# Four products in one PSUM bank without side sums, the second norm between the early products, the residual by another queue

## The chip, the cores and the metric

The kernel runs on one core of one Trainium2 chip. Its time is the device time of one launch in microseconds (us). TensorE (PE) multiplies, VectorE (DVE) and ScalarE (ACT) work on tiles and empty PSUM, GpSimd (POOL) does little, and SyncE (SP) issues the DMAs.

## The reference

Two layers over 1024 latent tokens of width 1024 (and 256 context tokens that layer 0 reads). Each layer is a mixer and then a channel MLP of hidden width 4096, both on a modulated norm and added to the stream with a gate:

```
x = x + g1 * mixer(modulate(rms_norm(x, n1), sh1, sc1))
x = x + g2 * sq_relu_mlp(modulate(rms_norm(x, n2), sh2, sc2), w1, w2)

def sq_relu_mlp(h, w1, w2):
    return jnp.square(jax.nn.relu(h @ w1)) @ w2
```

The mixer of layer 0 is retention beside softmax attention with shared keys and values; that of layer 1 is a gated MLP (`z = gelu(h @ w_in)`, `u, v = z`, `v` normed and mixed within chunks of 128 positions by a 128x128 matrix per group, then `(u * sv) @ w_out`). All is float32.

## The kernel before, in words

**Numbers.** Each float32 operand is split into a high part that PE takes and the rest (`split`: ACT casts the high part, DVE subtracts for the low part), and each product of two 128-wide tiles is three matmuls (`mm3`, lines 68 to 70): high by high, high by low, low by high. Tokens stand in the free dimension in two halves of 512 (`hf` 0 and 1).

**The channel MLP** (`layer_mlp`, line 903) replaces eight block products of a 2 by 2 blocked matrix product by seven. Activations come in seven forms (B11, T2, B21, T3, T1, T4, B22: halves of the tokens, and sums and differences of them), weights in seven (A11, S2, A12, S3, S1, A22, S4), which `w_forms` makes on DVE and ACT from two raw loads. A product (`block`) of four 128-wide tiles is 12 matmuls into one PSUM bank of 512 columns. There are eight banks in use as a ring.

`norm_forms` makes the normed activations: for half 0 the forms B11 and B21, for half 1 the other five, in four steps of the tile pairs t. It is a generator: `later` queues it, each `tick()` runs one step, `drain()` the rest. Half 0's steps run between the output projection's tiles of half 1. `up_first` then makes two products, A11 B11 and A12 B21, for the first eight of the 16 hidden blocks p (banks `uf`; results `ef`, `sf` go to DRAM by tiles of the ring `t`, four buffers that the norm uses too), and `drain()` after it runs half 1's norm. `mlp_up` makes the remaining products of each p in banks `ua`, `ub`, `ue`; seven forms of the result go to DRAM (`s_d`), and `mlp_down` loads them again and makes jobs (q, p0 to p1): q is one of four output block rows, a job takes one to four p. It accumulates into the residual tiles `xd` (the stream before the MLP, loaded from DRAM) by `scalar_tensor_tensor` on DVE; A11 B11, which three outputs share, is summed apart in a tile `acc` and added to three outputs in the last job of each q. The last three jobs, of p 13, 14 and 15, have three, two and one p. `done` then squares and sums the finished rows for the next norm, or writes the output.

**Queues and order.** All DMAs are issued on SP. Raw weights pass through three staging tiles of 512 KB, forms through a ring of 11 tiles `wr`. When the program is built, a scheduler sets each engine's order, which so differs from the code's in places; on the chip each engine runs its own in order and waits by semaphores.

Of the kernel before, what the change touches and what calls it, by code (L numbers as in the profile page):

```python
# [16 lines left out]
P = 128  # L17
D = 1024
KT = D // P
T = 1024  # L20
# [7 lines left out]
NW = 11  # L28
# [4 lines left out]
def hybrid_retention_gqa_chunkmlp_kernel(tc, I, out):  # L33
# [9 lines left out]
    stage, close_stage = open_pool("stage", bufs=3)  # L43
# [17 lines left out]

    def w_tile():

        wnext[0] += 1
        return wring[wnext[0] % NW]

# [9 lines left out]
    def load_w(src, name, eng=nc.vector):  # L76
        st = stage.tile([P, WCOL], F32, tag="st", name=f"st_{name}")
# [45 lines left out]
    def mod_steps(todo):  # L123
        for l, part in todo:
            acc = mpool[0].tile([P, D], F32, tag="macc", bufs=1, name=f"macc{l}{part}")
            for k in range(KT):
                st = stage.tile([P, WCOL], F32, tag="st", name=f"mw{l}{part}{k}")
# [432 lines left out]
    nt, close_nt = open_pool("nt")  # L560
    yf_pool, close_yf = open_pool("yf")
# [7 lines left out]
    def att_load(G, hh):  # L569
        if hh == 0:  # L570
# [4 lines left out]
            for dst, src in ((akc, ak_d[G, :, 0:TC]), (av[:, :, 0:1024], avd[:, 0:1024]), (av[:, :, 1024:], avd[:, 1024:])):  # L575
                st = stage.tile([P, WCOL], F32, tag="st", name=f"ast{G}")[:, :src.shape[-1]]
# [100 lines left out]
    def w_form(src, name, eng=nc.vector):  # L677
        w = src.shape[-1]
        t = w_tile().rearrange("p (a b) -> p a b", a=2)
        split(src, t[:, 0, :w], t[:, 1, :w], eng)  # L680
        return t

    def w_raw(src, name):
        n = src.shape[-2]
        r = stage.tile([P, WCOL], F32, tag="st", name=name)[:, :2 * n * P]
# [4 lines left out]
    def w_forms(src, name, skip=False, eng=nc.vector):  # L690
# [5 lines left out]
        if not skip:  # L696
            f["A11"] = w_form(R1[:, 0], f"w0_{name}")
        s1 = tmp(f"s1_{name}")[:, :w]
        eng.tensor_tensor(s1, R2[:, 0], R2[:, 1], ALU.add)
        s2 = tmp(f"s2_{name}")[:, :w]  # L700
        eng.tensor_tensor(s2, s1, R1[:, 0], ALU.subtract)
        f["S2"] = w_form(s2, f"w1_{name}")
        if not skip:
            f["A12"] = w_form(R1[:, 1], f"w2_{name}")
        eng.tensor_tensor(R2[:, 0], R1[:, 0], R2[:, 0], ALU.subtract)
        f["S3"] = w_form(R2[:, 0], f"w3_{name}")
        f["S1"] = w_form(s1, f"w4_{name}")
        f["A22"] = w_form(R2[:, 1], f"w5_{name}")
        eng.tensor_tensor(R1[:, 1], R1[:, 1], s2, ALU.subtract)
        f["S4"] = w_form(R1[:, 1], f"w6_{name}")  # L710
# [60 lines left out]
    def mlp_up(l, F, s_d, utemp, pro):  # L771
# [3 lines left out]
        for p in range(16):  # L775
# [9 lines left out]

            e1, s11 = utemp(f"e1_{l}_{p}"), utemp(f"s11_{l}_{p}")
            if p in pro:
# [8 lines left out]
            if p not in pro:  # L796
                block(a, f["A12"], F["B21"], False)
                nc.scalar.activation(s11, a, AF.Relu)
                nc.scalar.activation(s11, s11, AF.Square)
                put("B11", s11)  # L800
            block(b, f["S3"], F["T3"], False)
            u3 = utemp(f"u3_{l}_{p}")
            nc.vector.tensor_tensor(u3, b, e1, ALU.add)
            block(e, f["S1"], F["T1"], True)
            nc.vector.tensor_tensor(u3, e, u3, ALU.add)
            act(u3)
            put("B22", u3)
            block(b, f["A22"], F["T4"], False)
            nc.vector.tensor_tensor(e1, b, e1, ALU.add)
            act(e1)  # L810
# [9 lines left out]
            put("T3", u2)  # L820
            t4 = utemp(f"q4_{l}_{p}")
            nc.vector.tensor_tensor(t4, e1, t2, ALU.subtract)
            put("B21", e1)
            put("T4", t4)

    def up_first(l, F, s_d, e_d):

        for p0 in range(0, NPRO, 2):
# [17 lines left out]
    def mlp_down(l, xt, acc, s_d, done):  # L846
        S = {}
        sums = set()
# [10 lines left out]
        def job(q, p0, p1):  # L859
# [5 lines left out]
            f = w_forms(lambda i: I["w2"][l, q, i, :, :, p0:p1], name)  # L865
# [16 lines left out]
            block(a, f["A12"], F["B21"], False)  # L882
            stt(x11, a, g1)
            block(b, f["S3"], F["T3"], False)
            stt(x22, b, g2)
            block(e, f["S1"], F["T1"], True)
            stt(x22, e, g2)
            block(b, f["A22"], F["T4"], False)
            stt(x21, b, g2)
            block(e, f["S4"], F["B22"], False)  # L890
            stt(x12, e, g1)
# [7 lines left out]
        job(3, 0, 3)  # L899
        for i in range(16):  # L900
            job(i % 4, i, min(i + 4, 16))

    def layer_mlp(l, F, close_xt, s_d, e_d, x1_d, done):
# [9 lines left out]
        xt = [xd.tile([P, T], F32, name=f"xd{l}_{m}") for m in range(KT)]  # L913
        for m in range(KT):
            nc.sync.dma_start(xt[m], x1_d[m])
        acc = xd.tile([P, 4, H], F32, name=f"acc{l}")
        mlp_down(l, xt, acc, s_d, lambda q: done(q, xt))
        return close_xd, xt
# [20 lines left out]
    def done0(q, xt):  # L939
        if not ss1:  # L940
            ss1.extend(norm_tmp(0, 1))
        for m in (q, q + 4):
            for hf in range(2):
                norm_acc(nt, ss1[hf], xt[m][:, hf * H:(hf + 1) * H], m == 0, nc.vector)
            nc.sync.dma_start(xp_d[m], xt[m])

    close_xd, xt = layer_mlp(0, F, close_xa, s_d, e_d, x1_d, done0)
    hm = [[None] * KT for _ in range(2)]
    for hf in range(2):
        rs = norm_rstd(nt, ss1[hf], H)  # L950
# [20 lines left out]
    for cg in range(2):  # L971
        W = [load_w(I["wv"][cg, 2 * j:2 * j + 2].rearrange("k p n -> p k n"), f"wv{cg}_{j}") for j in range(4)]
        for tt in range(NTT):
            hf, o = tt // 4, (tt % 4) * P
            ps = mm_tile([P, 4, P], f"pv{cg}_{tt}")
            for k in range(KT):
                wc = slice((k % 2) * H, (k % 2) * H + H)
                mm3(ps.rearrange("p a b -> p (a b)"), hm[hf][k][:, 0, o:o + P], hm[hf][k][:, 1, o:o + P],
                    W[k // 2][0][:, wc], W[k // 2][1][:, wc], k == 0, k == KT - 1)
            for j in range(4):  # L980
                nc.scalar.activation(zg[cg * 4 + j][:, tt, :], ps[:, j, :], AF.Gelu_apprx_tanh)
# [12 lines left out]
    yg = [[None] * 8 for _ in range(2)]  # L994
    for g in range(8):
        W = load_w(I["wu"][g].rearrange("p k j -> p (k j)"), f"wu{g}")
        nc.vector.tensor_tensor(zg[g], zg[g], vr.unsqueeze(2).broadcast_to([P, NTT, P]), ALU.mult)
        for hf in range(2):
# [4 lines left out]
            pv = aux_tile([P, 4, P], f"psv{g}_{hf}")  # L1003
            for j in range(4):
                nc.tensor.matmul(pv[:, j, :], lhsT=zg[g][:, hf * 4 + j, :], rhs=wsT[:, g, :], start=True, stop=True)
            sv = tmp("sv").rearrange("p (a b) -> p a b", b=P)
            nc.vector.scalar_tensor_tensor(sv, pv, gains[:, 4, g:g + 1],
# [102 lines left out]
```

## Time and profile before

| | us |
|---|---|
| median of three runs (lowest, highest) | 2441.57 (2439.18, 2442.20) |
| the profiled execution | 2442.82 |
| its span, first to last instruction | 2440.5 |
| PE busy | 2248.6 (92%) |
| DVE busy | 1681.8 (69%) |
| ACT busy | 1021.3 (42%) |
| POOL busy | 123.8 (5%) |

Mean granted TensorE clock: 0.966 of full speed. Busy times are sums over the whole span, and the stages differ: in the up and down stages PE works nearly without a pause, and between stages it waits. A wait's releaser is the instruction whose end released the waiting one.

### The profile page before, as it was taken

How to read it: one execution, taken by the hardware profiler on the slowest of the kernel's cores; microseconds unless marked ns; L12 is line 12 of the kernel's file. 1: busy time of each engine (PE TensorE's matmuls, PEld its weight loads, DVE VectorE, ACT ScalarE, POOL GpSimd, SP SyncE). 2: the span in 40 equal slices, each digit the busy share in tenths (PEclk: the TensorE clock that was granted, in tenths of full speed). 3: DMA queues.
4: the chain of work that ended last, by engine and by line, in shares of the span. 5: the costliest groups of instructions: out<-in, count | busy, mean ns of one | idle time of the engine just before them, and what ended most of it. 6: DMA issues, size and time to landing. Idle time of an engine off the chain costs nothing. (4 is left out here: it accounts for less than half of the span.)

```text
span 2440.5 us, 28880 instructions
## 1 busy us (share of the span) xinstructions
PE 2248.6 (92%) x10412; PEld 1805.8 (74%) x10412; DVE 1681.8 (69%) x2798; ACT 1021.3 (42%) x1813; POOL 123.8 (5%) x101
## 2 busy tenths in 40 slices
PE   6998999799998699998999959999949999899998
PEld 1887787588886578876777838788837788677786
DVE  4657668689762977668878672444558766798886
ACT  3511122288644544554444233322445454544441
POOL 2223231000000000000000000000000000000000
PEclk9999999899999899999999969999979999999999
DMA  8245556410353464456444231115516544745442
GB/s 286 75 138 161 171 156 198 145 64 27 109 169 128 152 206 160 151 199 211 151 148 149 77 123 53 52 35 183 158 69 217 187 154 135 278 148 153 150 138 85
DMA packets 157407, 350.70 MB, mean 144 GB/s; under 512 B 16336, under 2 KB 30160, under 8 KB 157264
## 3 DMA queue, kind: packets, MB, share of 16 engines
q1 hardware_dynamic: 157264, 348.86, 44.3%
q8 instruction: 81, 1.33, 0.2%
q14 instruction: 62, 0.51, 0.1%
HBM read 262.29 MB, written 86.51 MB: 143 GB/s over the span
## 5 line engine op out<-in xcount | busy, mean ns | idle before, releaser
L68 PE MATMUL ub<-T,wr 128*128 128x512 f32 x384 | 153.8, 402 | 61.2 <-ACT wr L73 58.7
L68 PE MATMUL dbd<-sT,wr 128*128 128x512 f32 x384 | 155.9, 406 | 29.2 <-DVE xd L872 17.6
L68 PE MATMUL pl<-wr,h 128*128 128x512 f32 x384 | 154.1, 401 | 0.2 <-ACT zrl L477 0.2
L70 PE MATMUL dbd<-sT,wr 128*128 128x512 f32 x384 | 154.1, 401 | 0.0
L69 PE MATMUL dbd<-sT,wr 128*128 128x512 f32 x384 | 153.8, 400 | 0.0
L70 PE MATMUL ub<-T,wr 128*128 128x512 f32 x384 | 153.3, 399 | 0.0
L69 PE MATMUL ub<-T,wr 128*128 128x512 f32 x384 | 153.1, 399 | 0.0
L70 PE MATMUL pl<-wr,h 128*128 128x512 f32 x384 | 152.3, 397 | 0.0
L69 PE MATMUL pl<-wr,h 128*128 128x512 f32 x384 | 151.7, 395 | 0.0
L68 PEld LDWEIGHTS ub<-T,wr 128*128 128x128 f32 x384 | 73.1, 190 | 83.1 <-ACT wr L73 60.6
L73 ACT CAST wr<-ra_d 128x512 fp32r<-128x512 f32 (+3 forms) x114 | 62.4, 553 | 124.7 <-PE dbd L69 59.0
L68 PEld LDWEIGHTS dbd<-sT,wr 128*128 128x128 f32 x384 | 73.3, 191 | 53.9 <-DVE xd L872 20.0
L872 DVE SCALAR_TENSOR_TENSOR xd<-dbd,mcol,xd 128x512 f32<-128x512 f32 x114 | 85.2, 748 | 37.7 <-PE dbd L70 25.1
L132 DVE SCALAR_TENSOR_TENSOR macc<-mw,scc,macc 128x1024 f32<-128x1024 f32 x70 | 91.7, 1310 | 23.2 <-DMA mw<-in_mod_w 22.6
L68 PE MATMUL dad<-sB,wr 128*128 128x512 f32 x256 | 102.8, 402 | 5.2 <-ACT acc L878 3.4
L70 PE MATMUL dad<-sB,wr 128*128 128x512 f32 x256 | 101.6, 397 | 0.3 <-DVE wr L74 0.2
L69 PE MATMUL dad<-sB,wr 128*128 128x512 f32 x256 | 101.7, 397 | 0.0
L74 DVE TENSOR_TENSOR sT<-sT 128x512 fp32r<-128x512 f32 x128 | 87.4, 687 | 19.7 <-ACT sT L73 19.3
L73 ACT CAST sT<-sT 128x512 fp32r<-128x512 f32 x128 | 78.7, 619 | 48.5 <-DMA sT<-s_d 46.2
L70 PEld LDWEIGHTS dbd<-sT,wr 128*128 128x128 f32 x384 | 73.4, 191 | 18.9 <-DVE wr L74 1.1
L70 PEld LDWEIGHTS ub<-T,wr 128*128 128x128 f32 x384 | 72.9, 190 | 18.8 <-DVE wr L74 1.3
L69 PEld LDWEIGHTS dbd<-sT,wr 128*128 128x128 f32 x384 | 73.5, 192 | 16.5
(354 smaller groups left out, 6224.8 us busy)
## 6 DMA issues: line engine op xcount, KB each, us to landing
s_d<-ur SPq DMA_DIRECT2D x208, 256.0 KB, 2.2
mw<-in_mod_w SPq DMA_DIRECT2D x96, 512.0 KB, 4.5
sT<-s_d SPq DMA_DIRECT2D x128, 256.0 KB, 3.6
sB<-s_d SPq DMA_DIRECT2D x96, 256.0 KB, 2.7
st_wo<-in_wo SPq DMA_DIRECT2D x32, 512.0 KB, 3.9
ra_u<-in_w SPq DMA_DIRECT2D x32, 512.0 KB, 4.2
rb_u<-in_w SPq DMA_DIRECT2D x32, 512.0 KB, 3.8
ra_d<-in_w SPq DMA_DIRECT2D x26, 512.0 KB, 5.2
```

Of the source, the lines that this page charges most:

```text
L68: nc.tensor.matmul(ps, lhsT=a_hi, rhs=b_hi, start=first, stop=False, skip_group_check=more)
L69: nc.tensor.matmul(ps, lhsT=a_hi, rhs=b_lo, start=False, stop=False, skip_group_check=more)
L70: nc.tensor.matmul(ps, lhsT=a_lo, rhs=b_hi, start=False, stop=last, skip_group_check=more)
L73: nc.scalar.copy(hi, src)
L74: eng.tensor_tensor(lo, src, hi.bitcast(F32), ALU.subtract)
L132: nc.vector.scalar_tensor_tensor(acc, st, scc[:, k, 0:1], acc, ALU.mult, ALU.add)
L872: nc.vector.scalar_tensor_tensor(o, ps_, g, o, ALU.mult, ALU.add)
```

## The change

- The ring of weight forms has 12 tiles. Staging tiles are taken from a ring written out by hand, three, and a fourth from the attention on. The tile `acc` is gone.
- `up_first` calls `tick()` after each early product, so half 1's norm steps stand between the early products.
- `mlp_up`: for the eight p without early products, A11 B11, S2, S3 and A22 go into one bank (`ub`) in a chain, and the partial sums are copied out by ACT between them. The order of the forms is A11, A12, S2, S1, S3, S4, A22.
- `mlp_down`: the same chain; each partial sum is added to one output on its way, so no sum is kept apart. Half 0 of a row is finished (`done(q, 0)`) before half 1. For p 13 to 15 the S1 and S4 products are returned (`left`) and run later: in layer 0 between the two halves' norms, in layer 1 at the end.
- The residual is loaded on POOL's queue, and the residual for layer 1's mixer is written there in halves; the output is written in halves by SP.
- Layer 1's mixer: the first four tiles of `v` are summed with the input block outside, and the gate of `u` runs one product late.

```diff
@@ up_first
             for d in range(2):
                 block(ps[d], W[d][0], F["B11"], True)
+                tick()
                 e1 = tmp(f"ef{l}_{p0 + d}")
                 nc.scalar.copy(e1, ps[d])
                 nc.sync.dma_start(e_d[p0 + d], e1)
             for d in range(2):
                 block(ps[d], W[d][1], F["B21"], False)
+                tick()
@@ mlp_up
-                block(a, f["A11"], F["B11"], True)
-                nc.scalar.copy(e1, a)
-            block(b, f["S2"], F["T2"], True)
+                block(b, f["A11"], F["B11"], True)
+                nc.scalar.copy(e1, b)
+                block(a, f["A12"], F["B21"], True)
+                nc.vector.tensor_tensor(s11, a, e1, ALU.add)
+                act(s11)
+                put("B11", s11)
+            block(b, f["S2"], F["T2"], early)
             u2 = utemp(f"u2_{l}_{p}")
-            nc.vector.tensor_tensor(u2, b, e1, ALU.add)
...
+            if early:
+                nc.vector.tensor_tensor(u2, b, e1, ALU.add)
+            else:
+                nc.scalar.copy(u2, b)
+            block(e, f["S1"], F["T1"], True)
...
@@ mlp_down, job
-            block(a, f["A11"], F["B11"], True)
-            if q in sums:
-                nc.vector.tensor_tensor(acc[:, q, :], a, acc[:, q, :], ALU.add)
-            else:
-                nc.scalar.copy(acc[:, q, :], a)
-                sums.add(q)
-            block(b, f["S2"], F["T2"], True)
+            def p5():
+                block(e, f["S1"], F["T1"], True)
+                stt(x22, e, g2)
+
+            def p3():
+                block(e, f["S4"], F["B22"], False)
+                stt(x12, e, g1)
+                if p1 == 16:
+                    done(q, 1)
+
+            block(b, f["A11"], F["B11"], True)
+            stt(x11, b, g1)
+            block(a, f["A12"], F["B21"], True)
+            stt(x11, a, g1)
+            block(b, f["S2"], F["T2"], False)
             stt(x12, b, g1)
...
             if p1 == 16:
-                for o, g in ((x21, g2), (x12, g1), (x22, g2)):
-                    stt(o, acc[:, q, :], g)
-                done(q)
+                done(q, 0)
+            return (p5, p3) if keep else ()
@@ layer_mlp
-        for m in range(KT):
-            nc.sync.dma_start(xt[m], x1_d[m])
+        for m, x in xt.items():
+            nc.gpsimd.dma_start(x, x1_d[m])
@@ between the layers
     for hf in range(2):
+        if hf:
+            for g in left:
+                g()
         rs = norm_rstd(nt, ss1[hf], H)
```

PE, layer 0, around half 1's norm (`uf0_p` is the bank of an early product, the second name the activation form, `nsum` and `nbc` the norm's sum and broadcast). Before:

```order
L70 MATMUL uf0_7_6543<-B21_0_3_6209,wr9_73 128x512
L188 MATMUL nsum_6618<-ones_85,ss001_5711 128x1 x4
L198 MATMUL nbc_6627<-ident_80,rs_6625 128x128 x4
L68 MATMUL ub0_0_6773<-T2_0_0_6640,wr10_74 128x512
L69 MATMUL ub0_0_6773<-T2_0_0_6640,wr10_74 128x512
```

The same place in the changed kernel:

```order
L77 MATMUL uf0_0_6187<-B11_0_3_6082,wr9_76 128x512
L195 MATMUL nsum_6211<-ones_89,ss001_5600 128x1 x4
L75 MATMUL uf0_1_6188<-B11_0_0_5953,wr11_78 128x512
...
L205 MATMUL nbc_6235<-ident_84,rs_6218 128x128 x4
L75 MATMUL uf0_0_6187<-B21_0_0_5956,wr10_77 128x512
```

The norm's sum and broadcast have moved from behind the last of the 16 early products to behind the first and the second. The remaining first products (`uf0_2` to `uf0_7` with B11) come next, and then the second products.

ACT, layer 0, at the end of the early products (`ef` is the copy of a first product, `sf` the Relu and then the Square of both, `wr` the cast of a weight form). Before:

```order
L842 ACTIVATE sf0_5_6538<-uf0_5_6467 128x512
L843 ACTIVATE sf0_5_6538<-sf0_5_6538 128x512
L837 COPY ef0_6_6568<-uf0_6_6542 128x512
L837 COPY ef0_7_6583<-uf0_7_6543 128x512
L842 ACTIVATE sf0_6_6598<-uf0_6_6542 128x512
L843 ACTIVATE sf0_6_6598<-sf0_6_6598 128x512
L842 ACTIVATE sf0_7_6614<-uf0_7_6543 128x512
L843 ACTIVATE sf0_7_6614<-sf0_7_6614 128x512
L746 ACTIVATE xa0_5677<-xa0_5677,mcol03_1351 128x512
```

After:

```order
L861 ACTIVATE sf0_5_6519<-uf0_5_6450 128x512
L855 COPY ef0_6_6547<-uf0_6_6523 128x512
L862 ACTIVATE sf0_5_6519<-sf0_5_6519 128x512
L855 COPY ef0_7_6562<-uf0_7_6524 128x512
L80 CAST wr10_77<-st0_61 128x512
L861 ACTIVATE sf0_6_6577<-uf0_6_6523 128x512
L862 ACTIVATE sf0_6_6577<-sf0_6_6577 128x512
L861 ACTIVATE sf0_7_6593<-uf0_7_6524 128x512
L862 ACTIVATE sf0_7_6593<-sf0_7_6593 128x512
L80 CAST wr2_69<-s1_u0_0_6619 128x512
L80 CAST wr1_68<-s2_u0_0_6621 128x512
```

Behind the last `sf` stood the norm of half 1 (`xa0`); now the casts of the first weight forms of `mlp_up` stand there. PE makes `uf0_5` and `uf0_6` with B21 one right after the other now.

PE, the end of layer 0's MLP (`dbd0_q_p` and `ded0_q_p` are banks of the last jobs, `pv` the first product of layer 1's mixer). Before:

```order
L70 MATMUL ded0_3_15_11167<-sB22_0_15_10797,wr7_71 128x512
L188 MATMUL nsum_11213<-ones_85,ss010_10922 128x1 x4
L198 MATMUL nbc_11222<-ident_80,rs_11220 128x128 x4
L188 MATMUL nsum_11267<-ones_85,ss011_10923 128x1 x4
L198 MATMUL nbc_11276<-ident_80,rs_11274 128x128 x4
L68 MATMUL pv0_0_11357<-wr8_72,hm_0_0_11228 128x512
```

After:

```order
L77 MATMUL dbd0_3_15_10913<-sT4_0_15_10595,wr7_74 128x512
L195 MATMUL nsum_10943<-ones_89,ss010_10706 128x1 x4
L205 MATMUL nbc_10952<-ident_84,rs_10950 128x128 x4
L75 MATMUL ded0_1_13_10759<-sT1_0_13_10303,w3_d0_1_13_10745 128x512
...
L77 MATMUL ded0_3_15_10914<-sB22_0_15_10599,w5_d0_3_15_10907 128x512
L195 MATMUL nsum_11063<-ones_89,ss011_10707 128x1 x4
L205 MATMUL nbc_11072<-ident_84,rs_11070 128x128 x4
L75 MATMUL pv0_0_11149<-wr8_75,hm_0_0_10958 128x512
```

Between the first broadcast and the second sum now stand 36 matmuls, the S1 and S4 products of p 13, 14 and 15 that stood within their jobs before.

## Rows read from the trace of the kernel before

**Rows 1.** The page, part 1: busy time of each engine.

```profile
PE 2248.6 (92%) x10412; PEld 1805.8 (74%) x10412; DVE 1681.8 (69%) x2798; ACT 1021.3 (42%) x1813; POOL 123.8 (5%) x101
```

**Rows 2.** PE's waits: us in total, times, longest us.

```profile
PE ub L68 <- ACT wr L73: 58.7, 2, 29.4
PE dbd L68 <- DVE xd L872: 17.6, 9, 6.9
...
PE s L68 <- ACT wr L73: 14.4, 1, 14.4
...
PE psv L1005 <- DVE zg L997: 4.8, 1, 4.8
```

**Rows 3.** Busy us by stretch: length; PE, PEld, DVE, ACT, POOL; clock, DMA share, GB/s.

```profile
1120.00:1380.00 260.00, 258.70 (x1100) 205.86 (x1099) 211.31 (x333) 109.61 (x183) 0.00 (x0) 1.00 0.46 140
```

**Rows 4.** PE in order of time: start, duration, and idle before in brackets.

```profile
779.84 0.39 PE L69 MATMUL uf<-B,wr 128*128 128x512 f32 x1
780.07 0.40 PE L70 MATMUL uf<-B,wr 128*128 128x512 f32 x1
780.31 0.95 PE L188 MATMUL nsum<-ones,ss 128*128 128x1 f32 x8
782.59 1.16 PE L198 MATMUL nbc<-ident,rs 128*128 128x128 f32 x8 [1.34 <-POOL rs L192]
813.12 0.79 PE L68 MATMUL ub<-T,wr 128*128 128x512 f32 x1 [29.37 <-ACT wr L73]
```

**Rows 5.** DVE in the same manner.

```profile
737.66 0.69 DVE L182 TENSOR_TENSOR ss<-ss,sq 128x512 f32<-128x512 f32 x1 [0.16 <-ACT sq L181]
...
783.79 2.06 DVE L745 SCALAR_TENSOR_TENSOR xa<-xa,mcol,nbc 128x512 f32<-128x512 f32 x3 [2.34 <-PE nbc L198]
...
810.40 0.68 DVE L74 TENSOR_TENSOR B<-xa,B 128x512 fp32r<-128x512 f32 x1
811.01 0.69 DVE L699 TENSOR_TENSOR s_u<-rb_u 128x512 f32<-128x512 f32 x1
```

**Rows 6.** Stretches, columns as in rows 3.

```profile
740.00:780.00 40.00, 40.00 (x173) 32.12 (x172) 3.47 (x5) 15.31 (x26) 0.00 (x0) 1.00 0.40 136
...
1100.00:1120.00 20.00, 15.53 (x54) 11.54 (x55) 12.93 (x22) 6.60 (x14) 0.00 (x0) 0.75 0.86 334
```

**Rows 7.** ACT in order of time.

```profile
780.50 0.60 ACT L842 ACTIVATE sf<-uf 128x512 f32<-128x512 f32 x1 [1.54 <-PE uf L70]
781.13 0.63 ACT L843 ACTIVATE sf<-sf 128x512 f32<-128x512 f32 x1
...
811.73 1.34 ACT L73 CAST wr<-s_u 128x512 fp32r<-128x512 f32 x2 [2.03 <-DVE s_u L699]
```

**Rows 8.** All engines in order of time, from layer 0's up to its down stage.

```profile
1095.62 4.82 SPq L915 DMA_DIRECT2D xd<-x_d  x8
...
1103.33 0.75 DVE L872 SCALAR_TENSOR_TENSOR xd<-dbd,mcol,xd 128x512 f32<-128x512 f32 x1 [4.19 <-DMA xd<-x_d]
...
1104.14 0.80 PE L68 MATMUL dbd<-sT,wr 128*128 128x512 f32 x1 [6.92 <-DVE xd L872]
```

**Rows 9.** PE's waits from 2100 to 2122, the same place in layer 1.

```profile
PE dbd L68 <- DVE xd L872: 6.3, 1, 6.3
PE dad L68 <- ACT acc L878: 2.2, 1, 2.2
```

**Rows 10.** PE in order of time, end of layer 0.

```profile
1426.76 0.80 PE L68 MATMUL dbd<-sT,wr 128*128 128x512 f32 x1 [6.72 <-ACT wr L73]
...
1441.75 1.87 PE L188 MATMUL nsum<-ones,ss 128*128 128x1 f32 x8 [4.50 <-DVE ss L182]
...
1457.69 2.07 PE L198 MATMUL nbc<-ident,rs 128*128 128x128 f32 x8 [9.08 <-POOL rs L192]
```

**Rows 11.** DVE in order of time, the last row.

```profile
2434.72 1.41 DVE L872 SCALAR_TENSOR_TENSOR xd<-acc,mcol,xd 128x512 f32<-128x512 f32 x2
```

**Rows 12.** SP's DMA issues before the attention.

```profile
478.16 1.69 SPq L78 DMA_DIRECT2D st_aq<-aq_d  x2
```

More of the change, by code (lines that the diff above doesn't have):

```diff
@@ L42, in hybrid_retention_gqa_chunkmlp_kernel @@
     const, close_const = open_pool("const")
-    stage, close_stage = open_pool("stage", bufs=3)
+    stage, close_stage = open_pool("stage")
+    sring = [stage.tile([P, WCOL], F32, name=f"st{i}") for i in range(3)]
+    snext = [0]
     wpool, close_w = open_pool("wpool")
@@ L76, in load_w @@
     def load_w(src, name, eng=nc.vector):
-        st = stage.tile([P, WCOL], F32, tag="st", name=f"st_{name}")
+        st = st_tile()
         nc.sync.dma_start(st, src)
@@ L126, in mod_steps @@
             for k in range(KT):
-                st = stage.tile([P, WCOL], F32, tag="st", name=f"mw{l}{part}{k}")
+                st = st_tile()
                 nc.sync.dma_start(st, I["mod_w"][l, k * P:(k + 1) * P, part * D:(part + 1) * D])
@@ L684, in w_raw @@
         n = src.shape[-2]
-        r = stage.tile([P, WCOL], F32, tag="st", name=name)[:, :2 * n * P]
+        r = st_tile()[:, :2 * n * P]
         r = r.rearrange("p (j w) -> p j w", j=2)
@@ L688, in w_raw, with w_forms @@
         return r
[L690 removed]
+    def w_forms(src, name, skip=False, keep=False):
         R1 = w_raw(src(0), f"ra_{name}")
@@ L820, in mlp_up @@
             put("T3", u2)
+            block(b, f["A22"], F["T4"], False)
+            if early:
+                nc.vector.tensor_tensor(e1, b, e1, ALU.add)
+                act(e1)
+            else:
+                nc.scalar.activation(e1, b, AF.Relu)
+                nc.scalar.activation(e1, e1, AF.Square)
+            put("B21", e1)
             t4 = utemp(f"q4_{l}_{p}")
             nc.vector.tensor_tensor(t4, e1, t2, ALU.subtract)
-            put("B21", e1)
             put("T4", t4)
@@ L857, in load_s, with job @@
                 S[p][n] = o
-        def job(q, p0, p1):
+        def job(q, p0, p1, keep=False):
             for p in range(p0, p1):
@@ L899, in mlp_down @@
         job(3, 0, 3)
+        left = []
         for i in range(16):
-            job(i % 4, i, min(i + 4, 16))
+            left += job(i % 4, i, min(i + 4, 16), i > 12)
+        return left
     def layer_mlp(l, F, close_xt, s_d, e_d, x1_d, done):
@@ L912, in layer_mlp @@
         xd, close_xd = open_pool("xd", reuse_waits="tile")
-        xt = [xd.tile([P, T], F32, name=f"xd{l}_{m}") for m in range(KT)]
-        for m in range(KT):
-            nc.sync.dma_start(xt[m], x1_d[m])
-        acc = xd.tile([P, 4, H], F32, name=f"acc{l}")
-        mlp_down(l, xt, acc, s_d, lambda q: done(q, xt))
-        return close_xd, xt
+        xt = {m: xd.tile([P, T], F32, name=f"xd{l}_{m}") for m in (1, 5, 2, 6, 3, 7, 0, 4)}
+        for m, x in xt.items():
+            nc.gpsimd.dma_start(x, x1_d[m])
+        left = mlp_down(l, xt, s_d, lambda q, hf: done(q, hf, xt))
+        return close_xd, xt, left
     def scratch(l):
@@ L994, in hybrid_retention_gqa_chunkmlp_kernel, with gate @@
     yg = [[None] * 8 for _ in range(2)]
+    def gate(g, hf, u):
+        pv = aux_tile([P, 4, P], f"psv{g}_{hf}")
+        for j in range(4):
+            nc.tensor.matmul(pv[:, j, :], lhsT=zg[g][:, hf * 4 + j, :], rhs=wsT[:, g, :], start=True, stop=True)
+        sv = tmp("sv").rearrange("p (a b) -> p a b", b=P)
+        nc.vector.scalar_tensor_tensor(sv, pv, gains[:, 4, g:g + 1],
+                                       bsb[:, g, :].unsqueeze(1).broadcast_to([P, 4, P]), ALU.mult, ALU.add)
+        nc.vector.tensor_tensor(u, u, sv.rearrange("p a b -> p (a b)"), ALU.mult)
+        if hf == 0 and g < 4:
+            y = za.tile([P, 2, H], F32R, name=f"yg{g}_{hf}")
+        else:
+            y = f_tile(f"yg{g}_{hf}")
+        yg[hf][g] = y
+        split(u, y[:, 0, :], y[:, 1, :])
+    waits = []
     for g in range(8):
@@ L1002, in hybrid_retention_gqa_chunkmlp_kernel @@
             nc.scalar.activation(u, ps, AF.Gelu_apprx_tanh)
[L1003 to L1007, printed above, removed]
-                                           bsb[:, g, :].unsqueeze(1).broadcast_to([P, 4, P]), ALU.mult, ALU.add)
-            svf = sv.rearrange("p a b -> p (a b)")
-            nc.vector.tensor_tensor(u, u, svf, ALU.mult)
-            if hf == 0 and g < 4:
-                y = za.tile([P, 2, H], F32R, name=f"yg{g}_{hf}")
-            else:
-                y = f_tile(f"yg{g}_{hf}")
-            yg[hf][g] = y
-            split(u, y[:, 0, :], y[:, 1, :])
+            waits.append((g, hf, u))
+            if len(waits) > 1:
+                gate(*waits.pop(0))
+    gate(*waits.pop(0))
     close_gp()
@@ L1036, in close_xb @@
         close_za()
-    close_xd, xt = layer_mlp(1, F, close_xb, s_d, e_d, x1_d, done1)
+    close_xd, xt, left = layer_mlp(1, F, close_xb, s_d, e_d, x1_d, done1)
+    for g in left:
+        g()
     close_xd()
```

114 lines of the change are left out of this document (62 added, 52 removed).

## The prediction

> **What bounds the kernel now.** I read the page's first part, then TensorE's (PE's) list of waits, then the stretches around the longest waits in order of time. The page says PE is busy 92% of the span [rows 1], VectorE 69% of it. So the kernel is PE-bound, and the number of matmuls does not change; what there is to win is in PE's idle time, 2440.5 - 2248.6 = 192 us. The list of waits [rows 2] shows where a large part of it lies: 58.7 us in only two waits of `ub`, the first product of the up stage, one per layer; 17.6 us where a product of the down stage waits for an addition into the residual tile `xd`; 14.4 us before the attention scores; 4.8 us of the gate product. Away from these places nothing is left to win: from 1120 to 1380, the middle of layer 0's down stage, PE is busy 258.70 of 260 us [rows 3]. So the change is priced place by place.
>
> **Second half's norm between the early products (both layers).** One matmul of 512 columns follows the last every 0.233 us, a product of 12 takes 2.80 us. The last early product ends at 780.31, then come the norm's sum and broadcast (0.95, a wait of 1.34, 1.16), and then PE stands still for 29.37 us until 813.12 [rows 4]. VectorE (DVE) shows why: 44 operations of the norm from 783.79 to 811.08, back to back at 0.6 us, and behind them the weight forms from 811.01 on [rows 5]. They could have run earlier: the sum of squares that the norm needs is complete at 737.66 + 0.69 = 738.35 [rows 5], the 16 early products begin at 780.31 - 16 x 2.80 = 735.5, and of the 40 us from 740 to 780 DVE works 3.47 [rows 6]. So there is room for the norm's 27.3 us, and in the new order it stands there: sum after the first early product, broadcast after the second (about 743.3), and after the last two weight splits that go ahead of it the norm runs from about 744 to 772.
>
> What is late next is ScalarE (ACT), not DVE. In the new order ACT's copy `ef` of a first product, which must precede the second product in the same bank, stands behind work that comes late: `ef0_2` behind the activation of the norm's eighth tile (about 766.5, 35 of the 44 DVE operations after 744); `ef0_4` behind the Relu of `uf0_3`, and `ef0_6` behind the Relu of `uf0_5`, that is, behind products that PE has only just finished. Relu, Square and a copy of this size take 0.6 us each [rows 7]. With about 0.2 us for each hand-over, `ef0_2` costs about 1.1 us, `ef0_4` and `ef0_6` 1.4 each, `ef0_1` 0.3. At the end the casts of the first weight forms stand behind Relu and Square of `uf0_7`: 0.2 + 0.60 + 0.63 + 1.34 for the two casts [rows 7] = 2.7. The first `ub` then starts at 780.31 + 2.1 (sum and broadcast, now inside) + 4.2 + 2.7 = 789.3 instead of 813.12: 23.8 us earlier. The first matmuls after the long wait are recorded at 0.79 us where 0.39 is usual [rows 4], and a wait of 2.7 us should cost less of that: about 1 us more. I take 25 us per layer, 50 in all; the second wait is as long as the first (58.7 in two, longest 29.4). Bounds per layer: 32 (no stall at all) and 15 (the ring of four temporaries, which the norm now shares with the early products' copies and their writes, stalls each of the last six pairs by 1.5 us more).
>
> **Residual by another queue (both layers).** In layer 0 SyncE issues the eight loads of `xd` at 1095.62, taking 4.82 us, DVE's first addition gets its tile at 1103.33 after 4.19 us of waiting, and the product that needs the bank back starts at 1104.14 after 6.92 us [rows 8]. The tiles are free earlier (the up stage's last buffers are freed one by one), and on GpSimd's queue the loads no longer stand behind the writes of the up stage. Layer 1 has the same wait, 6.3 us, and 2.2 for the copy of the side sum, which falls away [rows 9]. I take 6.5 us in each, 13. Bounds: 0 and 10 each (with the slow first matmuls behind the wait). Here the Trainium skill speaks against the change: "DMA: Bandwidth & Descriptors", section "Issuing engines are not separate DMA queues", says that DMAs of all issuing engines run interleaved on the same 16 DMA engines, and that another issuer saves only the issuing time. The trace gives that weight: from 1100 to 1120 the DMA engines are 0.86 busy [rows 6]. By the rule 13 would shrink to at most the issue time, 2 x 4.82 = 9.6. By the row on the wait, what counts is when the loads may start, and I keep 13.
>
> **End of layer 0.** PE waits 6.72 us for a weight cast at 1426.76, 4.50 for the sum of squares at 1441.75, and 9.08 for the broadcast of half 1's norm at 1457.69 [rows 10]; that one is long because half 0's eight tiles stand before it in the program, DVE making each in two operations. The change defers 36 matmuls (six short chains of the last three jobs, 36 x 0.233 = 8.4 us) and puts them between the norms of half 0 and half 1. They cover 8.4 of the 9.08 us. But they are taken from before, where they covered evacuations of the short jobs, and the first product of the next mixer still stands behind half 1's broadcast, whose sum needs them. Twelve additions of the side sums go per layer (0.70 us each by [rows 11], 2 x in 1.41), of which only those of the last job lie on the path. I take a gain of 4 us, half of 8.4; bounds -5 (each of the six chains shows its 0.75 us addition) and +12 (8.4 and the last job's additions and part of 4.50). The reciprocal root on GpSimd now stands behind 12 to 16 half-size writes of the residual in its queue; what issuing one there costs no row shows. From below it is 0, from above the 0.6 us that SyncE takes per load (4.82 / 8, [rows 8]), times the last four: 2.4 us, within the bound.
>
> **End of layer 1.** The last addition ends at 2434.72 + 1.41 = 2436.1, 4.4 us before the span's end, and it is the third of three that add side sums [rows 11]. Afterwards one addition follows the last matmul, and the writes are halves. Gain: two or three additions (2 us) and about 1 us of the write: 3 (bounds 1 to 5).
>
> **Gate delayed by one product:** the single wait of 4.8 us [rows 2] is covered by a product of 5.6 us (24 matmuls): 5, bounds 2 and 6.
>
> **Start of attention.** The 14.4 us before the scores [rows 2] end when the query tile is cast; its load was issued at 478.16 [rows 12], when the three staging tiles came free. With a fourth staging tile the queries are loaded and cast earlier. The context keys are still cast at about 477, and the softmax, which fills DVE and ACT in this stage, needs their scores, so only half is kept: 6, bounds 0 and 12.
>
> **Side sums, chain in one bank, ACT copies.** In the steady stages I take 0. Per up step without early products DVE loses two operations and ACT gains two copies; the bank that takes the four-product chain is read three times between products, and each time a product of 2.80 us in another bank stands between, against an addition of 0.75 [rows 8] or a copy of 0.6. Before there were also three such turns per step. The Trainium skill's "Perfetto Trace Analysis", section "Optimizing Tensor Performance", would have independent products rotate through different banks so that the evacuation of one overlaps the next; the row on 1120 to 1380 shows PE full with chains of this kind, and the sum by the rule would be that of the third rival. Bounds: +3 (waits of 0.2 to 1.4 us that stand there today) and -10.
>
> **The sum.** 50 + 13 + 4 + 3 + 5 + 6 = 81 us off the profiled execution's 2442.8 (span 2440.5 and 2.3 around it), 2361.8; that execution lies 1.25 above the median of the runs, 2441.57, so 2360.5, said as 2360.
>
> **Rivals.**
> 1. The norm does not fit: the shared ring of four temporaries and ACT's strict order spread the norm over more than the early products, and each layer saves only the lower bound of 15. For: ACT works 20 norm casts and 8 activations at 0.6 us beside 24 operations of the early products, all in one order. Against: DVE was idle for 36 of 40 us. Time: 2360 + 2 x 10 = 2380.
> 2. The residual's new queue brings nothing, because the DMA engines are full there (0.86) and weights wait instead: 13 us fewer, and layer 0's end 2 later: 2375. By the Trainium skill's rule on issuing engines alone it would be 3 us fewer, 2364.
> 3. Slower than before: the chain in one bank shows its evacuations. Where DVE or ACT, each in strict order, comes 2 us late to a bank, PE waits. There are about 3 turns x 21 full steps x 2 layers = 126 turns; from 81 / 126 = 0.64 us each the whole gain is eaten; at 0.75, one whole addition per turn, it is 2360 + 95 = 2455. Against: one product of 2.80 us stands in each turn, and the same number of turns exists now with 1.3 us of idleness in 260.
> 4. The schedule is better than I read it: no stall in the early products and the attention fully moved: 2360 - 14 - 6 = 2340.
>
> **How the numbers follow.** Forecast 0.52, rival 1 0.16, rival 2 0.12, rival 3 0.04, rival 4 0.16. The forecast's own range, with its unknown terms pulling apart, is about 2350 to 2372. The range of 8 in 10 reaches down through most of rival 4, to 2336, and up past rivals 1 and 2, to 2392. A measurement of this kernel can tell 0.2%, 5 us. Everything but rival 3 is far beyond that: faster 0.95, within 0.2% 0.01, slower 0.04.
>
> **What would show it.** In the profile after, the two waits of `ub` of 29 us should be gone, with a few waits of 1 to 3 us of `uf` and `ub` for ACT in their place, and DVE busy for most of what was 740 to 780. The wait of the down stage's first products for `xd` should be under 1 us in both layers. At layer 0's end the 36 deferred matmuls should stand where the 9.08 us were. PE's busy time should stay at 2248 within a few us. If the `ub` waits are still over 10 us each, or new waits of `ub`, `ue`, `dbd` for ACT or DVE appear with counts of dozens in the steady stages, the forecast is wrong.

## The result and the profile after

The changed kernel takes 2381.52 us (median of four runs, 2380.79 to 2382.32) against 2441.65 of the kernel before: a ratio of 0.9756, 95% interval 0.9739 to 0.9773. The forecast was 2360, range 2336 to 2392: the time lies in the range, and of the 81 us forecast 60 came.

The page after, part 1, against [rows 1]:

```profile
PE 2254.3 (95%) x10412; PEld 1810.1 (76%) x10412; DVE 1651.0 (69%) x2750; ACT 1028.3 (43%) x1837; POOL 144.1 (6%) x133
```

PE has as many matmuls and is busy for nearly as long (5.7 us more); its idle time fell from 192 to 126 us. PE's waits after, in the same columns as [rows 2]:

```profile
PE dbd L75 <- DVE xd L890: 23.5, 10, 8.9
...
PE ded L75 <- DVE xd L890: 10.2, 6, 4.7
PE nsum L195 <- DVE ss L189: 8.9, 2, 5.2
...
PE s L75 <- ACT akc L80: 6.3, 1, 6.3
PE uf L75 <- ACT ef L855: 6.0, 6, 1.2
PE ub L75 <- ACT wr L80: 4.8, 2, 2.4
```

The 58.7 us of `ub` are 4.8, with 6.0 of `uf` beside them, and the 4.8 of `psv` are gone. But the down stage's wait for `xd`, 17.6 before, has grown to 23.5, with 10.2 of `ded` beside it (2.7 before). To see what each place brought, I cut both traces at the same matmuls (us; job 13 is the first of the last three):

| stretch | before | after | gained | forecast |
|---|---|---|---|---|
| start to the last projection product | 467.2 | 470.3 | -3.1 | 0 |
| attention, to the first output projection | 176.5 | 171.0 | 5.5 | 6 |
| layer 0: output projection | 91.8 | 91.8 | 0 | 0 |
| layer 0: first early to first up product | 77.6 | 53.0 | 24.6 | 25 |
| layer 0: up stage | 272.8 | 272.4 | 0.4 | 0 |
| layer 0: down stage to job 13 | 301.0 | 300.5 | 0.5 | 6.5 |
| job 13 to the first product of v | 72.5 | 73.5 | -1.0 | 4 |
| v | 88.9 | 90.8 | -1.9 | 0 |
| u and the gates | 111.1 | 103.8 | 7.3 | 5 |
| layer 1: output projection | 91.2 | 91.2 | 0 | 0 |
| layer 1: first early to first up product | 77.7 | 53.0 | 24.7 | 25 |
| layer 1: up stage | 273.3 | 272.2 | 1.1 | 0 |
| layer 1: down stage to job 13 | 300.4 | 302.5 | -2.1 | 6.5 |
| job 13 to the end | 38.4 | 34.5 | 3.9 | 3 |

The first line is not the change's: ten profiles of kernels that are alike up to there (the changed one and nine of the experiments) need 467.1 to 475.6 us for it. Because of this scatter the experiments below are compared by stretch, and by total time only where the difference is large. A scatter of some 2 to 3 us stands in other stretches too: in kernels that are alike there, v takes 88.7 to 91.6 us.

The place of [rows 4], PE in order of time (start, duration, idle before in brackets):

```profile
763.88 0.50 PE L75 MATMUL uf<-B,wr 128*128 128x512 f32 x1 [0.66 <-ACT ef L855]
770.91 0.50 PE L75 MATMUL uf<-B,wr 128*128 128x512 f32 x1 [1.16 <-ACT ef L855]
777.94 0.50 PE L75 MATMUL uf<-B,wr 128*128 128x512 f32 x1 [1.16 <-ACT ef L855]
786.17 0.71 PE L75 MATMUL ub<-T,wr 128*128 128x512 f32 x1 [2.38 <-ACT wr L80]
```

DVE there, the norm's first and last row, against [rows 5]:

```profile
740.99 2.06 DVE L752 SCALAR_TENSOR_TENSOR xa<-xa,mcol,nbc 128x512 f32<-128x512 f32 x3
...
767.93 0.69 DVE L81 TENSOR_TENSOR B<-xa,B 128x512 fp32r<-128x512 f32 x1
```

And ACT, at the first and at the third of PE's four waits:

```profile
762.63 0.72 ACT L753 ACTIVATE xa<-xa,mcol 128x512 f32<-128x512 f32 x1 [1.56 <-DVE xa L752]
763.26 1.05 ACT L855 COPY ef<-uf 128x512 f32<-128x512 f32 x2
...
776.81 0.60 ACT L861 ACTIVATE sf<-uf 128x512 f32<-128x512 f32 x1 [1.53 <-PE uf L77]
777.31 0.58 ACT L855 COPY ef<-uf 128x512 f32<-128x512 f32 x1
```

The norm runs for 27.6 us beside the products, and what PE waits for now are copies: the first stands behind the activation of the norm's last tile (0.66), the next two behind the Relu of the product just finished (1.16 each). Then come 2.38 for the casts at the end.

The down stage of layer 0, against [rows 8], all engines in order of time.

```profile
1042.54 1.63 POOL L940 DMA_DIRECT2D xd<-x_d  x3 [18.01 <-DMA s_d<-ur]
...
1065.78 1.21 SPq L695 DMA_DIRECT2D st<-in_w  x2
...
1066.64 2.13 POOL L940 DMA_DIRECT2D xd<-x_d  x4 [22.47 <-DMA s_d<-ur]
...
1071.08 0.51 ACT L80 CAST wr<-st 128x384 fp32r<-128x384 f32 x1 [1.48 <-DMA st<-in_w]
1071.62 0.56 DVE L81 TENSOR_TENSOR wr<-st,wr 128x384 fp32r<-128x384 f32 x1 [1.29 <-ACT wr L80]
1072.10 0.74 DVE L890 SCALAR_TENSOR_TENSOR xd<-dbd,mcol,xd 128x512 f32<-128x512 f32 x1
...
1072.90 0.79 PE L75 MATMUL dbd<-sT,wr 128*128 128x512 f32 x1 [7.92 <-DVE xd L890]
```

Four of the residual's tiles are loaded in time, and still PE waits 7.92 us instead of 6.92. Now the addition that PE waits for stands on DVE behind a weight split of the third job, and that weight's load, issued at 1065.78, is there for the cast only at 1071.08; and the stretch (length; PE, PEld, DVE, ACT, POOL; clock, DMA share, GB/s) shows full DMA engines:

```profile
1066.00:1082.00 16.00, 7.14 (x18) 4.86 (x19) 9.73 (x17) 6.61 (x13) 2.13 (x4) 0.68 1.01 362
```

The end of layer 0, against [rows 10]: PE, then DVE.

```profile
1414.95 0.80 PE L75 MATMUL ded<-sB,w_d 128*128 128x512 f32 x1 [4.68 <-DVE xd L890]
...
1427.41 1.87 PE L195 MATMUL nsum<-ones,ss 128*128 128x1 f32 x8 [5.19 <-DVE ss L189]
1430.72 2.07 PE L205 MATMUL nbc<-ident,rs 128*128 128x128 f32 x8 [1.44 <-POOL rs L199]
```

```profile
1412.83 1.40 DVE L983 SCALAR_TENSOR_TENSOR hp<-xd,mcol,nbc 128x512 f32<-128x512 f32 x2
1414.14 0.75 DVE L890 SCALAR_TENSOR_TENSOR xd<-ded,mcol,xd 128x512 f32<-128x512 f32 x1
...
1423.49 3.87 DVE L189 TENSOR_TENSOR ss<-ss,sq 128x512 f32<-128x512 f32 x5
```

The 9.08 us of the second broadcast are gone, and in their place stand 4.68 for a deferred product, whose bank is emptied only behind half 0's norm tiles on DVE, and 5.19 for a sum of squares that can't be complete before the deferred products are added.

### The profile page after: what moved, and what is told of

Read it like the earlier page. It is cut to its first block, busy times and chain, and to the rows that moved or that the text cites. A ratio compares the mean times of both kernels' runs of the same rounds, so it can differ in the third digit from the quotient of the medians.

```text
span 2380.5 us, 28904 instructions
## 1 busy us (share of the span) xinstructions
PE 2254.3 (95%) x10412; PEld 1810.1 (76%) x10412; DVE 1651.0 (69%) x2750; ACT 1028.3 (43%) x1837; POOL 144.1 (6%) x133
## 4 chain that ended last, share of the span: by engine, by line
PE 78%; DVE 9%; DMA 6%; ACT 3%; issue 2%; POOL 1%; SPq 0%; DVEq 0%; ACTq 0%; POOLq 0%
PE dbd L75 5%; PE ub L75 4%; PE dbd L77 4%; PE dbd L76 4%; PE ub L76 4%; PE ub L77 4%; PE po L76 3%; PE po L77 3%; PE po L75 2%; PE ue L75 2%; PE ue L77 2%; PE ue L76 2%; PE ded L75 2%; PE ded L76 2%; PE ded L77 2%; PE pl L77 2%
## 5 line engine op out<-in xcount | busy, mean ns | idle before, releaser
L80 ACT CAST wr<-st 128x512 fp32r<-128x512 f32 (+4 forms) x422 | 281.0, 672 | 509.3 <-PE dbd L76 84.2
L81 DVE TENSOR_TENSOR wr<-st,wr 128x512 fp32r<-128x512 f32 (+4 forms) x418 | 310.3, 748 | 183.7 <-ACT wr L80 142.6
L75 PE MATMUL dbd<-sT,wr 128*128 128x512 f32 x384 | 157.1, 409 | 30.3 <-DVE xd L890 23.5
L890 DVE SCALAR_TENSOR_TENSOR xd<-dbd,mcol,xd 128x512 f32<-128x512 f32 x152 | 113.1, 748 | 46.9 <-PE dbd L77 46.7
L75 PEld LDWEIGHTS dbd<-sT,wr 128*128 128x128 f32 x384 | 73.5, 191 | 58.2 <-DVE xd L890 29.8
L139 DVE SCALAR_TENSOR_TENSOR macc<-st,scc,macc 128x1024 f32<-128x1024 f32 x70 | 92.8, 1325 | 23.6 <-DMA st<-in_mod_w 23.0
L75 PEld LDWEIGHTS ub<-T,wr 128*128 128x128 f32 x384 | 72.4, 189 | 26.9 <-ACT wr L80 6.1
L81 DVE TENSOR_TENSOR sB<-sB 128x512 fp32r<-128x512 f32 x96 | 66.0, 688 | 31.6 <-ACT sB L80 31.4
L77 PEld LDWEIGHTS ub<-T,wr 128*128 128x128 f32 x384 | 72.7, 189 | 18.0
L76 PEld LDWEIGHTS ub<-T,wr 128*128 128x128 f32 x384 | 72.6, 189 | 17.5
```

What stands on the lines that cost most here:

```text
L75: nc.tensor.matmul(ps, lhsT=a_hi, rhs=b_hi, start=first, stop=False, skip_group_check=more)
L76: nc.tensor.matmul(ps, lhsT=a_hi, rhs=b_lo, start=False, stop=False, skip_group_check=more)
L77: nc.tensor.matmul(ps, lhsT=a_lo, rhs=b_hi, start=False, stop=last, skip_group_check=more)
L80: nc.scalar.copy(hi, src)
L81: eng.tensor_tensor(lo, src, hi.bitcast(F32), ALU.subtract)
L890: nc.vector.scalar_tensor_tensor(o, ps_, g, o, ALU.mult, ALU.add)
```

## The experiments

**Is the gain at `ub` the norm's alone?** The kernel before, with only this:

```diff
                 block(ps[d], W[d][0], F["B11"], True)
+                tick()
...
                 block(ps[d], W[d][1], F["B21"], False)
+                tick()
```

> The kernel before with one edit: half 1's norm steps run between the early products (a step after each product); nothing else of the change. Theory: the whole gain at the two ub waits comes from this edit and needs no other part of the change. Stage from the first early product to the first up product: 77.6 us before, 53.0 in the changed kernel; here 53 +-2 in both layers, time 2441.6 - 49 = 2392 (2389 to 2396). Rival: the other parts help it (order of the weight forms, a twelfth form tile, so the norm is not held behind weight forms): stage of 58 us or more, time over 2402.

Measured: 2392.62 us (ratio 0.9803, 0.9771 to 0.9835), 48 less than the kernel before on the same chip; the stage takes 56.6 and 56.7 us. The stage lies between the two expectations (53 and 58), the time in the theory's range. So this edit carries most of it: 21 of the 24.6 us per layer. The rest is a wait that the changed kernel doesn't have:

```profile
768.81 0.80 PE L70 MATMUL uf<-B,wr 128*128 128x512 f32 x1 [5.31 <-DVE wr L74]
...
794.63 0.50 PE L68 MATMUL ub<-T,wr 128*128 128x512 f32 x1 [2.38 <-ACT wr L73]
```

A weight split of the early products stands behind the norm on DVE here. Which of the other edits (the twelfth form tile, the fourth staging tile) takes it away was not tried.

**Why did the residual's term not come?** First, the changed kernel without the residual:

```diff
-            nc.gpsimd.dma_start(x, x1_d[m])
+            nc.gpsimd.memset(x, 0.0)
```

> The changed kernel without the residual's loads into the down stage (the eight tiles are set to zero by GpSimd instead; the residual is left out of the sum). Theory A (the first jobs' weights come late, since their staging tiles come free late, and the additions stand behind their splits on VectorE): the first long wait of dbd for VectorE, 7.9 us in layer 0 and 8.9 in layer 1, stays at 6 or more, time 2377 to 2382. Theory B (the residual's 4 MB fill the DMA engines just when the weights are wanted): the wait falls to 3 us or less in each layer and the time to 2371 or less.

Measured: 2363.63 us (0.968, 0.9661 to 0.9698). PE at the start of layer 0's down stage:

```profile
1064.77 0.50 PE L75 MATMUL dbd<-sT,wr 128*128 128x512 f32 x1 [1.52 <-DVE xd L890]
1068.60 0.80 PE L75 MATMUL dbd<-sB,wr 128*128 128x512 f32 x1 [2.88 <-ACT wr L80]
```

The long wait is gone in both layers; the first 126 matmuls of the down stage take 37.4 and 38.1 us instead of 42.4 and 43.4. Theory B's numbers came, but they don't show its cause, since the edit changed DVE's order as well. The same place in this run, all engines:

```profile
1062.69 1.22 SPq L695 DMA_DIRECT2D st<-in_w  x2
...
1063.97 0.74 DVE L890 SCALAR_TENSOR_TENSOR xd<-dbd,mcol,xd 128x512 f32<-128x512 f32 x1
...
1068.04 0.93 ACT L80 CAST wr<-st 128x384 fp32r<-128x384 f32 x2 [0.47 <-DMA st<-in_w]
```

The first addition stands in front of the weight split here, not behind it. And the weights come hardly sooner: from issue to cast it is 5.35 us here and 5.30 in the changed kernel (5.68 and 6.23 in layer 1), with DMA engines as full (share 0.95 from 1063 to 1068 here, 0.96 from 1065 to 1070 there). I estimate from these rows that in the old order PE would have waited some 6.6 us here: the cast at 1068.04, then 1.8 us from the cast to PE as in the changed kernel, after a product that ended at 1063.25. By this estimate most of the fall of the wait is due to DVE's order, which is theory A. How much of the 5 us of the stretch is due to the bytes stays open.

Then four of the eight tiles later, each pair behind the weights of its job:

```diff
-        for m, x in xt.items():
-            nc.gpsimd.dma_start(x, x1_d[m])
+        for m in (1, 5, 2, 6):
+            nc.gpsimd.dma_start(xt[m], x1_d[m])
...
+            if q not in loaded:
+                loaded.add(q)
+                for m in (q, q + 4):
+                    nc.sync.dma_start(xt[m], x1_d[m])
```

> The changed kernel; of the residual's eight tiles only the four for the first two jobs are loaded by GpSimd, the other four by SyncE, each pair right behind the weights of the job that first needs it. Without any residual load the first 126 matmuls of the down stage took 37.4 and 38.1 us (layers 0 and 1) instead of 42.4 and 43.4. Theory B (2 MB of residual issued at one time hold back the third job's weights): 39 to 40 us in each layer, time 2372 to 2377. Theory A (the weights are late whatever else is loaded, the order on the queues is of no use): 42 us or more, 2380 or more.

Measured: 2374.11 us (0.9721, 0.9701 to 0.9742), 41.9 and 40.0 us. The time and layer 1's stretch are in theory B's ranges, layer 0's stretch is nearly theory A's, and the wait stayed in both layers; in layer 1:

```profile
2053.97 0.80 PE L75 MATMUL dbd<-sT,wr 128*128 128x512 f32 x1 [8.07 <-DVE xd L895]
```

So later loads alone don't cure the wait. The two versions at the end of this section contain the same edit and settle the rest: their stretches are 40.2 and 39.2, 39.7 and 39.9 us, while the five kernels with all eight loads as in the changed one (itself and four of the experiments) need 42.2 to 44.5 in their ten stretches. So the edit gains some 3 us per layer, layer 0 in this run being the exception. The wait is still 7.5 to 9.0 us in all six stretches, 7.3 to 10.0 in those ten; so much of the gain lies behind it.

Last, all eight loads by SyncE again, in the changed order of tiles:

```diff
-            nc.gpsimd.dma_start(x, x1_d[m])
+            nc.sync.dma_start(x, x1_d[m])
```

> The changed kernel with the residual's eight loads issued by SyncE again, in the changed order of tiles. Theory (the bytes that must pass the 16 DMA engines around the start of the down stage decide, not the issuer): the first 126 matmuls take 42 to 44.5 us in each layer (42.4 and 43.4 as changed), time 2379 to 2385. Rival (GpSimd's four early tiles do save DMA time at the boundary, and SyncE's order puts them in front of the third job's second weight tile): 46 us or more in each layer, 2387 or more.

Measured: 2372.56 us (0.9709, 0.9692 to 0.9726), 41.2 and 40.7 us. Neither: taking GpSimd's queue away is not equal but better, 1.2 and 2.7 us in these stretches, both below all ten stretches with the eight loads by GpSimd, and 1.8 and 3.3 in the up stages before them (270.6 and 268.9 us instead of 272.4 and 272.2). At the end of layer 1's up stage the changed kernel has a row that this one lacks, with 0.81 us at the same place in layer 0:

```profile
2040.57 0.50 PE L75 MATMUL ub<-T,wr 128*128 128x512 f32 x1 [1.48 <-DVE ur L818]
```

This wait is missing only here and in the run without the residual; every other version of the changed kernel has it in both layers, with 0.7 to 1.9 us. The other 1.8 us of layer 1's up stage are slow matmuls at its start, which come and go (last section). So the queue brought nothing and cost some 6 us: 3.9 in the stretches and 2.3 at the ends of the up stages. By what means it costs them no run shows. The rule of the Trainium skill that the prediction weighed ("DMA: Bandwidth & Descriptors", "Issuing engines are not separate DMA queues") agrees with the runs as far as it goes, since another issuer brought no gain (2381.52 us by GpSimd, 2372.56 by SyncE); the 13 us that I kept against it did not come.

**Why did the end of layer 0 gain nothing?** The products of p 13 to 15 left in their jobs in layer 0:

```diff
-            left += job(i % 4, i, min(i + 4, 16), i > 12)
+            left += job(i % 4, i, min(i + 4, 16), i > 12 and l == 1)
```

> The changed kernel, but in layer 0 the S1 and S4 products of p 13 to 15 stay within their jobs (layer 1 as changed). From the start of job 13 to the first product of v it is 72.6 us in the kernel before and 73.4 in the changed one. Theory: the deferral moves waits and saves none, since its chains' additions stand behind half 0's norm tiles on VectorE: 72 to 75 us here too, time 2380 to 2384. Rival: the deferral did save the 8.4 us of its matmuls and something else in the tail lost as much: 79 us or more, time 2387 or more.

Measured: 2367.33 us (0.9692, 0.9668 to 0.9716). Job 13 to v takes 60.9 us. My theory and the rival both fell: the deferral is not neutral and saves nothing, it costs 12.6 us here, a little more than the 11.6 that the rest of the change gains. The largest part of that gain is in PE's waits for weight casts from job 13 to v, first in the kernel before, then in this run:

```profile
PE dbd L68 <- ACT wr L73: 10.3, 2, 6.7
...
PE ded L75 <- ACT wr L80: 3.7, 2, 3.2
```

Then deferred as before, but in front of both norms:

```diff
+    for g in left:
+        g()
     for hf in range(2):
-        if hf:
-            for g in left:
-                g()
         rs = norm_rstd(nt, ss1[hf], H)
```

> The changed kernel; in layer 0 the deferred products of p 13 to 15 run before both halves' norms instead of between them. From the start of job 13 to the first product of v: 73.4 us as changed, 60.9 with the products left in their jobs. Theory: the deferral costs because its six additions, the last squares and so half 1's sum stand behind half 0's 16 norm operations on VectorE; in front of them they don't: 60 to 64 us, time 2368 to 2372. Rival: taking the products out of the short jobs costs by itself, since their evacuations lose cover: 68 us or more, 2376 or more.

Measured: 2369.74 us (0.97, 0.9675 to 0.9725); job 13 to v 59.6 us. The theory holds: taking the products out of the short jobs costs nothing, placing them behind half 0's norm does. PE's two last waits are again those of [rows 10]:

```profile
1409.42 1.87 PE L195 MATMUL nsum<-ones,ss 128*128 128x1 f32 x8 [3.03 <-DVE ss L189]
1420.74 2.07 PE L205 MATMUL nbc<-ident,rs 128*128 128x128 f32 x8 [9.46 <-POOL rs L199]
```

That 9.46 can be filled with work that needs half 0 alone. The changed kernel with the first four tiles of v in front of half 1's norm:

```diff
     for hf in range(2):
         if hf:
             for g in left:
                 g()
+            for k in range(KT):
+                for tt in range(4):
+                    v_mm(0, tt, k)
         rs = norm_rstd(nt, ss1[hf], H)
...
```

> The changed kernel, with the first four tiles of v (96 matmuls, 22 us) issued between half 0's norm and half 1's. Theory: in the tail PE lacks work that half 0 alone allows, since v stands behind half 1's broadcast; its waits of 4.7, 5.2 and 1.4 us there and some slow matmuls go: time 2368 to 2372. Rival: VectorE's chain through both halves' norm tiles (22 us) sets the end of the stage, and what PE does earlier it waits for later: time 2378 to 2382.

Measured: 2367.84 us (0.9694, 0.9674 to 0.9714). As v moves, the measure is job 13 to the first product of u: 72.5 + 88.9 = 161.4 before, 164.3 as changed, 152.5 with the products left in place, 148.9 with them in front, 150.7 here. These last three differ by no more than v's scatter of 3 us. The time lies just below the theory's 2368 to 2372.

**The copies at the early products.**

```diff
-                nc.scalar.copy(e1, ps[d])
+                (nc.scalar.copy if p0 < 4 else nc.vector.tensor_copy)(e1, ps[d])
```

> The changed kernel; the copies of the first products of p 4 to 7 are made by VectorE instead of ScalarE (both layers). Theory: the waits of uf for ACT, 6.0 us in six, are copies that stand in ACT's order behind the Relu of a product just finished; four of the six go: 2.4 us or less left, first early to first up product 50.7 +-0.5 us instead of 53.0, time 2376 to 2379. Rival: PE loses the same time one step later (the weight forms follow the copies on VectorE, and ub waits longer): 53 us, 2381.

Measured: 2379.2 us (0.9736, 0.9712 to 0.976); the stage takes 51.2 us in both layers, 1.8 less. PE's waits of `uf`:

```profile
PE uf L75 <- DVE ef L855: 1.5, 2, 0.7
PE uf L75 <- ACT ef L855: 1.3, 2, 0.7
```

2.8 us in place of 6.0: the mechanism is shown, at slightly under its expected size; the time alone, 2.3 us less, could not tell it from no change.

**All together.** The four edits, as in the diffs above (products left in place, v between, residual late, copies by DVE):

```diff
+                (nc.scalar.copy if p0 < 4 else nc.vector.tensor_copy)(e1, ps[d])
...
+            if q not in loaded:
...
+            left += job(i % 4, i, min(i + 4, 16), i > 12 and l == 1)
...
+                for tt in range(4):
+                    v_mm(0, tt, k)
```

> The changed kernel with four edits: layer 0's S1 and S4 products left in their jobs, the first four tiles of v between the two halves' norms, four residual tiles loaded late, the four copies by VectorE. Theory (the terms add: 12.5 for the deferral, up to 9 for the wait of half 1's broadcast, 7 for the residual, 4 for the copies): 2346 to 2354. Rival: the first two remove the same wait, about 13 us between them: 2356 to 2360.

Measured: 2354.95 us (0.9647, 0.9622 to 0.9671), just above the theory's range and just below the rival's. By stretch the rival is right: job 13 to u is 148.7 us, 15.6 less than as changed, not the sum of 11.8 and 13.6.

The same with the deferred products in front of both norms instead of in their jobs:

```diff
-            left += job(i % 4, i, min(i + 4, 16), i > 12 and l == 1)
+            left += job(i % 4, i, min(i + 4, 16), i > 12)
...
+    for g in left:
+        g()
     for hf in range(2):
         if hf:
-            for g in left:
-                g()
...
```

> The version with all four edits, but layer 0's deferred products run before both halves' norms rather than in their jobs. Job 13 to the first product of u takes 148.7 us with them in their jobs and 148.9 with them in front and v not moved. Theory (in front they fill the last jobs' waits, and v between the norms then hides half 1's broadcast): 144 to 147 us, time 2350 to 2354. Rival (VectorE's additions, squares and norm tiles set the end in both): 148 to 150, 2355 to 2358.

Measured: 2350.38 us (0.9624, 0.9609 to 0.9638), the lowest median of all, below both kernels; by time alone it can't be told from the version before it, whose interval overlaps. Job 13 to u takes 47.2 + 93.7 = 140.9 us, better than either expectation. PE's waits from 1358 to 1501:

```profile
PE dbd L75 <- DVE xd L895: 3.6, 3, 1.9
PE pv L75 <- ACT hm L1006: 3.2, 2, 1.6
PE nbc L205 <- POOL rs L199: 2.5, 1, 2.5
PE nsum L195 <- DVE ss L189: 2.4, 1, 2.4
```

These four lines are together 11.7 us, where half 1's broadcast alone took 9.08 in the kernel before.

## Why the prediction was right, and where it was not

- **The norm between the early products.** Right, in mechanism and size: 24.6 and 24.7 us for 25 each. Room on DVE, norm in 27 us, then copies in ACT's order; the stalls are 0.66, 1.16, 1.16 and 2.38, where I had 1.1, 1.4, 1.4 and 2.7. No row shows the 0.2 us that I gave to each hand-over; at the third stall the copy ends at 777.89 and PE starts at 777.94. Rival 1 (15 per layer) is out.
- **Residual by another queue.** Wrong, the larger error: 13 us forecast, 0.5 - 2.1 = -1.6 measured over the two stretches to job 13. The failed step is "what counts is when the loads may start". Half of the loads do start earlier, but an early tile releases nothing while the addition into it stands on DVE behind the third job's weight split: PE waits 7.92 and 8.88 us where it waited 6.92 and 6.28. Rival 2 was right in that weights are waited for instead, and its price, 13, is what was missed at this place. Its reason, full DMA engines, is only argued: the share is 1.01 and the row with 0.86 in [rows 6] had hinted at it, but the first of these weights lands as long after its issue without the residual. What the runs do show is 5 us per layer without the residual, where DVE's order differs too, some 3 for loading half of it later, and some 6 in all that GpSimd's queue costs over SyncE's.
- **End of layer 0.** Wrong: 4 forecast, -1.0 measured. The step that failed is the cover: I let 36 matmuls cover 8.4 us of a wait without following their additions. They stand behind half 0's norm tiles on DVE, and half 1's sum stands behind them. The bound of -5 held it, but named the wrong cause. Without the deferral the same change gains 11.6 there, 6.6 of it in waits for weight casts, which the prediction named (6.72) but gave no gain; which edit shortens them no run separates.
- **Gate, end of layer 1, attention.** Right in sign and near in size: 7.3 for 5, 3.9 for 3, 5.5 for 6. The gate's 7.3 lies above its bound of 6, since slow matmuls went with the wait: in the kernel before the granted clock was 0.87 from 1560 to 1575, behind the wait, and in the changed one 1.00 throughout. The wait for the scores became a wait of 6.3 for the context keys, as forecast.
- **Steady stages.** Right at 0. From the 127th matmul to job 13 the down stage of layer 0 takes 258.1 us, 257.9 before, and from 1100 to 1341 PE is busy 238.99 of 241. It waits 2.0 us there, 1.3 in the 260 us of [rows 3], so the four-product chain in one bank exposes next to nothing, and rival 3 is out:

```profile
1100.00:1341.00 241.00, 238.99 (x1019) 190.73 (x1018) 197.95 (x313) 104.07 (x173) 0.00 (x0) 1.00 0.49 146
```

The missing 21 us are 14.6 of the residual, 5 of layer 0's end and 3.1 of the first stage, which lie within its scatter; the remaining stretches are together 1.6 better than forecast. The range held the time only because it was drawn up past rivals 1 and 2, to 2392; the forecast's own range ended at 2372.

## What to carry to other kernels

An engine idle beside a long chain is room only if everything that feeds and follows the chain is followed through the fixed orders of all engines: here ACT's order set the remaining waits to within half a microsecond. Work deferred to fill a gap brings its own evacuation with it, and the gap is filled only if that evacuation is not queued behind what the gap was waiting for; better fill it with work that nothing at that place waits for. Before you load a tile earlier, look at what else the instruction that waits for it stands behind; and where the DMA engines are full, ask which bytes can come later before you look at queues. When an experiment takes work out of a kernel, check that the order of the rest is still the same.

## What the runs showed of the hardware

- From 1066 to 1082 the 16 DMA engines moved 362 GB/s at a share of 1.01; a GpSimd issue of 512 KB is recorded with about 0.53 us (2.13 for four).
- After the same wait of 2.4 us before the up stage the first matmuls of `ub` were slow in some executions and not in others: 0.71 for the first in the changed kernel (clock 0.97 over the next 64 us), 0.50 in the one with the norm alone. In 9 of the 22 up stages behind such a wait the granted clock of the first 8 us was 0.79 to 0.81, in the others 1.00. That is 1 to 2 us of an up stage's length that no edit explains.
- Behind the 4.68 us of waiting at layer 0's end the granted clock was 0.50 from 1415 to 1420, the lower of its two levels (1.2 GHz), with matmuls recorded at 0.63 instead of 0.39. Over the whole stretch, which has other waits before and after, it was 0.66:

```profile
1400.00:1433.00 33.00, 20.24 (x68) 16.76 (x68) 19.81 (x32) 8.92 (x14) 5.36 (x8) 0.66 0.24 89
```
